# A mixture of experts whose tokens are gathered for two experts at a time, and an eighth weight buffer

## The chip, the cores and the metric

The kernel runs on one core of a Trainium2 chip. The metric is the device time of one execution in microseconds (us). The profile names the engines PE (TensorE, matmul; PEld are its weight loads, which overlap), DVE (VectorE), ACT (ScalarE), POOL (GpSimd) and SP (SyncE, which here only issues transfers).

## The reference

Three transformer blocks of width 1024 run one after another on one sequence of 256 tokens. Only the end of the third, a mixture of 32 experts of which each token uses four, bears on the change:

```python
def moe_ffn(h, router_w, router_b, w1, b1, w2, b2):
    logits = (h @ router_w + router_b).astype(jnp.float32)
    top_val, top_idx = lax.top_k(logits, TOP_K)      # 4 of 32
    gate = jax.nn.softmax(top_val, axis=-1)
    ...                                              # tokens are sorted by expert
    def block_ffn(args):
        xb, e = args
        act = clamped_swiglu(xb @ w1[e] + b1[e])     # 1024 -> 2 x 1024 -> 1024
        return act @ w2[e] + b2[e]                   # 1024 -> 1024
    ...
    contrib = gate_sorted[:, None].astype(h.dtype) * y_buf[dest]
    return jnp.zeros((T, D), h.dtype).at[sorted_tok].add(contrib)
```

All is float32. One expert's weights are 12 MB (8 for w1, 4 for w2), so all 32 are 384 MB that have to be read once.

## The kernel before

The blocks 1 and 2 and the mixer of block 3 take the first 1.7 ms and are not touched. `moe` then sorts the experts by how many tokens chose them. The first four in this order (`BIGS = 4`) are "large" and get up to 128 slots for tokens, the other 28 are "small" and get 64 (`SMALLS`). What doesn't fit is done by a fallback at the end, under a condition.

**Precision.** A float32 product is made of one-pass products of type `F32R`, on values split in a high and a low part. Weights: `split` (L507) copies a buffer of 1 MB ([128, 2048]) to `whi` on ScalarE (L509) and puts the difference into `wlo` on VectorE (L510). A large expert takes three products for each buffer (x high with w high, x high with w low, x low with w high); a small one puts the high and the low parts of its 64 tokens side by side in 128 columns and takes two. For a small expert one buffer in `up` and one in `down` (k == 1) is not split but multiplied as it is, as a plain float32 matmul.

**The loop.** Round r (0 to 31) runs `up(r)`, the first product of expert r (8 buffers, slots 0 to 7 of the round), and then `down` (4 buffers, slots 8 to 11) of the expert one (large) or two (small) earlier. The order on TensorE, ScalarE and VectorE is the order in which the program writes the instructions. All side work is put into slots: `at(r, slot, f)` says behind which buffer of which round `f` is written, and `pair_of(step, r, slot, behind)` writes a step's matmuls in a slot and its copy out of PSUM `behind` slots later. Such side work is the activation of the last pair of experts (`take`, `fold`, `activate`, `silu`, `gated`, `turn`), weighing the results by the gates (`weigh`), adding them to the tokens (`combine`), and the gather of the next experts' tokens.

**The gather.** `gather(r, n)` (L1753) makes the inputs of `n` experts from expert r on. `G` is a one-hot matrix (tokens by slots), built on VectorE. For each of 8 chunks of 128 features, `chunk(k)` multiplies the tokens (`hh` high, `hl` low, two halves of tokens each: four matmuls, each with weights of its own) by `G`, into one PSUM tile `gp` of the two `aux` banks, and ScalarE copies `gp` to `gx`. The matmuls' moving side is all `n` experts at once: 2 x 128 or 4 x 64, 256 columns. `scatter` transposes `G` of one expert for the way back and picks the gates. The calls: `gather(0, 2)` ahead of the loop (L1966), `gather(2, 2)` in one piece between `up(0)` and the bias products of round 0 (L2038 to L2040), `gather(4, 4)` in the slots of round 3, and from round 6 on `gather(r + 2, 4)` in every fourth round, slots 8 to 11 and then 0 to 7 of the next round.

**The weight buffers.** `raw` inside `moe` (L1794) issues each transfer of 1 MB on SyncE's queue, in order, into seven buffers in turn: five of tag `raw`, then `rawm`, then `rawx`. A transfer waits until the buffer's last readers are done. `gx` has three buffers of 8 KB per partition; the staging tile `braw` of the bias (L1969) uses one of them before its turn.

Of the kernel before, what the change touches and what calls it, by code (L numbers as in the profile page):

```python
# [12 lines left out]
F32 = mybir.dt.float32  # L13
F32R = mybir.dt.float32r
BF16 = mybir.dt.bfloat16
AF = mybir.ActivationFunctionType
# [10 lines left out]
UNIT = 1024  # L27
WAIT = 6
RAWS = 5
BIGS = 4  # L30
SMALLS = 64
# [294 lines left out]
class Norm:  # L326

    urgent = warm = False
    tag = "aux"
# [105 lines left out]
class Net:  # L435
# [1202 lines left out]
    def moe(s, x, nm, ctx):  # L1638


        nc, I = s.nc, s.I
        mm = nc.tensor.matmul
        mod = s.mods["wmod"]
        mp = ctx.enter_context(s.tc.tile_pool(name="mp", bufs=1))
# [64 lines left out]
        for t in range(2):  # L1709
            for i in range(2):  # L1710
                p = aux("htp", (128, 4, 128))
# [12 lines left out]
        p = aux("gatp", (128, 2, 128))  # L1724
# [4 lines left out]
        p = aux("gater", W)  # L1729
# [5 lines left out]
        X, GT, GS, Y, A = {}, {}, {}, {}, {}  # L1735
# [14 lines left out]
                nc.vector.tensor_reduce(GS[r], g, axis=AX.X, op=ALU.add)  # L1750
            return out

        def gather(r, n):  # L1753


            G = mp.tile([128, 2, n, 128], F32R, name="G", tag="G", bufs=1)
            slots, w = ("iota", 128) if n == 2 else ("twice", SMALLS)
            for t in range(2):
                for a in range(n):
                    nc.vector.tensor_scalar(G[:, t, a], k_(slots), pos[:, t, r + a:r + a + 1], None,  # L1760
                                            op0=ALU.is_equal)
            xg = [mp.tile([128, 8, 2, 128], F32R, name="gx", tag="gx", bufs=3) for _ in range(2)]
            for a in range(n):
                X[r + a] = (xg[a][:, :, 0], xg[a][:, :, 1]) if n == 2 else xg[a // 2][:, :, a % 2]

            def chunk(k):
                p = aux("gp", (128, n, 2, w))
                for i, src in enumerate((hh, hl)):
                    for t in range(2):
                        mm(p[:, :, i], src[:, t, k * 128:(k + 1) * 128], G[:, t, :, 0:w], start=t == 0,  # L1770
                           stop=t == 1)

                def out():
                    for a in range(2):
                        q = p[:, a] if n == 2 else p[:, 2 * a:2 * a + 2].rearrange("p a b c -> p a (b c)")
                        nc.scalar.activation(xg[a][:, k], q, AF.Copy)
                return out
            return [lambda k=k: chunk(k) for k in range(8)] + [lambda a=a: scatter(r + a, G[:, :, a])
                                                               for a in range(n)]

# [12 lines left out]

        def raw(ap):  # L1794

            s.turn = (s.turn + 1) % (RAWS + 2)
            if s.turn > 1:
                return s.raw(ap)
            if s.turn:
                w = s.xp.tile([128, 2 * UNIT], F32, name="rawx", tag="x", bufs=2)  # L1800
            else:
                w = mp.tile([128, 2 * UNIT], F32, name="rawm", tag="rawm", bufs=1)
            nc.sync.dma_start(w, ap)
            return w
        s.turn = 1

        def parts(what, r, k):

# [25 lines left out]
        def pair_of(step, r, slot, behind=2):  # L1834

            at(r, slot, lambda: at(r, slot + behind, step()))
# [126 lines left out]
            o = acc[:, 2 * c2:2 * c2 + 2]  # L1963
            return lambda: nc.vector.tensor_add(o, o, p)  # L1964

        for f in gather(0, 2):  # L1966
            f()()
        b1 = mp.tile([128, 1024], F32R, name="b1")
        b = mp.tile([128, 1024], F32, name="braw", tag="gx", bufs=3)  # L1969
        nc.scalar.dma_start(b, I["b1"])  # L1970
        b2 = s.xp.tile([32, 1024], F32, name="b2", tag="macc", bufs=1)
        nc.scalar.dma_start(b2, I["b2"])
# [22 lines left out]
        for r in range(32):  # L1995
            q = r - 1 if r < BIGS else r - 2

            d = {0: (), 1: (), BIGS: (BIGS - 2,), BIGS + 1: (), BIGS + 2: (BIGS - 1,)}.get(
                r, (r - 2,) if r < BIGS else (r - 3,))
            for z in d:  # L2000
                at(r, 1, lambda z=z: weigh(z, 0))
                at(r, 2, lambda z=z: weigh(z, 1))
                if z % 2:
                    for c2 in range(4):
                        pair_of(lambda z=z, c2=c2: combine(z - 1, c2), r, 4 + c2, 1)
            t = r - 1 if r <= BIGS else r - 2 if r % 2 == 0 else -1
            if t >= 0:
                at(r, 0, lambda t=t: activate(t))
                at(r, 1, lambda t=t: silu(t))
                at(r, 2, lambda t=t: gated(t))  # L2010

                def turned(t=t, r=r):
                    out = turn(t)
                    at(r, 6, lambda: out(0))
                    at(r, 7, lambda: out(1))
                at(r, 3, turned)
            if r != 0:
                at(r, 9 if r == BIGS else 10, lambda r=r: take(r))
                at(r, 9 if r == BIGS else 10, lambda r=r: fold(r, 0))
                at(r, 9 if r == BIGS else 11, lambda r=r: fold(r, 1))  # L2020
            if r == 3 or r % 4 == 2 and BIGS < r < 30:
                g = r + 1 if r == 3 else r + 2
                spots = [(3, k) for k in range(12)] if r == 3 else (
                    [(r, 8 + k) for k in range(4)] + [(r + 1, k) for k in range(8)])

                def begin(g=g, spots=spots):
                    for f, (rr, k) in zip(gather(g, 4), spots):
                        if (rr, k) == spots[0]:
                            at(rr, k + 2, f())
                        else:  # L2030
                            pair_of(f, rr, k)
                at(*spots[0], begin)
        order_ = s.tc.manual_schedule(engines={mybir.EngineType.PE, mybir.EngineType.Activation,
                                               mybir.EngineType.DVE})
        with order_:
            for r in range(32):
                up(r)
                if r == 0:  # L2038
                    for f in gather(2, 2):
                        f()()  # L2040
                    for c2 in range(4):
                        bias2(c2)
                    take(0)
                    for k in range(8, 12):
                        run(0, k)
                elif r < BIGS or r > BIGS + 1:
                    for _ in down(r - 1 if r < BIGS else r - 2, r):
                        pass
                elif r == BIGS:
                    half = down(BIGS - 1, r)  # L2050
                    next(half)
                    next(half)
                    run(r, 10)
                    run(r, 11)
                else:
                    run(r, 8)
                    run(r, 9)
                    for _ in half:
                        pass
                    run(r, 10)  # L2060
                    run(r, 11)
            activate(30)
            silu(30)
            weigh(29, 0)
            weigh(29, 1)
            gated(30)
            out = turn(30)
            for c2 in range(4):
                combine(28, c2)()
                if c2 % 2:  # L2070
                    out(c2 // 2)
            for _ in down(30, 32):
                pass
            xr = mp.tile([128, 8, T], F32, name="xr", tag="ml", bufs=1)
            nc.scalar.dma_start(xr, xd)
            d = down(31, 33, "up")
            next(d)
            weigh(30, 0)
            next(d)
            weigh(30, 1)  # L2080
            next(d)
            for c in range(8):
                nc.vector.scalar_tensor_tensor(acc[:, c], acc[:, c], g2(c), xr[:, c], op0=ALU.mult,
                                               op1=ALU.add)
            for _ in d:
                pass
            p = s.bank("cbl", (128, 4, 256), "p2", 1)
            ps = [p[:, 0:2], p[:, 2:4], aux("cbl", (128, 2, 256)), aux("cbl", (128, 2, 256))]
            for c in range(8):
                back(ps[c // 2][:, c % 2], c, (30,), c % 2 == 0, False)  # L2090
            weigh(31, 0)
            weigh(31, 1)
            for c in range(8):
                back(ps[c // 2][:, c % 2], c, (31,), False)
                nc.vector.scalar_tensor_tensor(acc[:, c], ps[c // 2][:, c % 2], g2(c), acc[:, c],
                                               op0=ALU.mult, op1=ALU.add)
                if c % 2:
                    nc.sync.dma_start(s.O["out"][:, c - 1:c + 1], acc[:, c - 1:c + 1])
# [49 lines left out]
    def past(s, mp, pgd, shift, acc, iota, hh, hl, g2):  # L2148
        nc, I = s.nc, s.I
# [3 lines left out]
        with s.tc.For_i(0, 32) as e:  # L2153
# [7 lines left out]
            q = aux("gto", (128, 2, 128))  # L2161
# [4 lines left out]
            q = aux("gso", (128, 1))  # L2166
            for t in range(2):
                mm(q, G[:, t], c4[:, 2 + t:3 + t], start=t == 0, stop=t == 1)
            nc.vector.tensor_copy(gs, q)
            xg = mp.tile([128, 8, 128], F32, name="xo", tag="gx", bufs=3)  # L2170
            for k in range(8):
                q = aux("xo", (128, 128))
                ks = slice(k * 128, k * 128 + 128)
# [34 lines left out]
            for k in range(8):  # L2208
                q = aux("bto", (128, 128))
# [61 lines left out]
```

## Time and profile before

| | us |
|---|---|
| median of 3 runs | 2808.79 |
| lowest and highest of them | 2794.71 and 2810.84 |
| the profiled execution, its own time | 2793.71 |
| its span in the trace | 2791.9 |

The profile is one execution. The page gives the busy time of each engine; the windows give it by stretch, with TensorE's granted clock (1.00 is full speed), the share of time that the transfers were busy, and their rate. The chain of work that ended last goes back from the last instruction: at each step to what released it, or to the instruction before it on its engine; "issue" in it is time in which the engine waited for nothing that the profile shows. Where two pieces of the chain follow each other without a gap on one engine, that engine set the pace there. The mixture of experts runs from some 1690 us to the end; the large experts up to about 1860 us.

### The profile page before, as it was taken

The page shows a single profiled execution, that of the slowest core. Times are in us where ns is not written, and L with a number is a line of the kernel's source. Part 1 is how long each engine was busy: PE and PEld are TensorE (multiplying, and loading weights), DVE is VectorE, ACT ScalarE, POOL GpSimd, SP SyncE. Part 2 cuts the span into 40 slices and gives each one's busy share as a digit, 9 for nine tenths or more (in the row PEclk, how much of TensorE's full clock was granted, in tenths as well). Part 3 has the DMA queues.
Part 4 walks back from the last instruction along what each step waited for, and adds up shares of the span by engine and source line. Part 5 has one row for each costly group of instructions (what it writes and reads, how often), then busy time and mean ns, then how long its engine had stood idle before and what let it go on. Part 6 is the DMA issues. An engine that isn't in the chain of part 4 may idle for free. (4 is left out here: it accounts for less than half of the span.)

```text
span 2791.9 us, 45884 instructions
## 1 busy us (share of the span) xinstructions
PE 2717.9 (97%) x17764; PEld 2364.8 (85%) x17764; DVE 2245.2 (80%) x3537; ACT 1683.1 (60%) x2658; POOL 3.3 (0%) x10
## 2 busy tenths in 40 slices
PE   9999999999999999999999998999999999999996
PEld 9999999999988999889999866877776767676764
DVE  7776777787776778888777754989999899999995
ACT  6554454464544545664467645777777777777773
POOL 0000000000000000000000000000000000000000
PEclk9999999999999999999999998999999999999998
DMA  7664466666653666437632333989999999999994
GB/s 290 229 227 166 173 221 240 244 224 242 227 182 122 236 243 225 150 139 256 234 142 96 111 118 120 359 306 384 395 405 395 398 402 389 405 387 400 388 413 161
DMA packets 102433, 728.97 MB, mean 261 GB/s; under 512 B 11384, under 2 KB 12920, under 8 KB 14528
## 3 DMA queue, kind: packets, MB, share of 16 engines
q1 hardware_dynamic: 99648, 719.64, 67.0%
q10 hardware_dynamic: 2560, 6.32, 0.7%
q8 instruction: 143, 2.34, 0.3%
q14 instruction: 82, 0.67, 0.1%
HBM read 723.80 MB, written 2.11 MB: 260 GB/s over the span
## 5 line engine op out<-in xcount | busy, mean ns | idle before, releaser
L510 DVE TENSOR_TENSOR wlo<-raw,whi 128x512 fp32r<-128x512 f32 (+1 forms) x1238 | 1178.7, 990 | 199.8 <-ACT whi L509 195.7
L509 ACT ACTIVATE whi<-raw 128x512 fp32r<-128x512 f32 (+1 forms) x1238 | 1006.6, 867 | 518.3 <-issue 283.1
L515 PE MATMUL gu<-xh,whi 128*128 128x256 f32 (+1 forms) x1760 | 499.7, 284 | 2.1 <-ACT whi L509 2.1
L517 PE MATMUL gu<-xh,wlo 128*128 128x256 f32 (+1 forms) x1760 | 497.6, 283 | 0.7 <-DVE wlo L510 0.7
L516 PE MATMUL gu<-xl,whi 128*128 128x256 f32 (+1 forms) x1760 | 498.1, 283 | 0.0
L515 PEld LDWEIGHTS gu<-xh,whi 128*128 128x128 f32 x1760 | 332.4, 189 | 2.9 <-ACT whi L509 2.5
L517 PEld LDWEIGHTS gu<-xh,wlo 128*128 128x128 f32 x1760 | 333.8, 190 | 1.1 <-DVE wlo L510 0.9
L516 PEld LDWEIGHTS gu<-xl,whi 128*128 128x128 f32 x1760 | 332.9, 189 | 0.3
L1848 PE MATMUL p<-whi,gx 128*128 128x512 f32 x1040 | 289.0, 404 | 2.5 <-ACT whi L509 2.5
L1848 PE MATMUL p<-wlo,gx 128*128 128x512 f32 x912 | 259.7, 407 | 23.6 <-DVE wlo L510 21.0
L517 PE MATMUL acc<-fh,wlo 128*128 128x256 f32 x880 | 245.5, 280 | 0.0
L516 PE MATMUL acc<-fl,whi 128*128 128x256 f32 x880 | 245.0, 280 | 0.1
L515 PE MATMUL acc<-fh,whi 128*128 128x256 f32 x880 | 242.4, 280 | 0.0
L1848 PEld LDWEIGHTS p<-whi,gx 128*128 128x128 f32 x1040 | 195.1, 189 | 54.5 <-issue 7.4
L1848 PEld LDWEIGHTS p<-wlo,gx 128*128 128x128 f32 x912 | 158.0, 189 | 78.7 <-DVE wlo L510 54.8
L516 PEld LDWEIGHTS acc<-fl,whi 128*128 128x128 f32 x880 | 165.8, 188 | 0.6 <-DVE fl L510 0.4
L517 PEld LDWEIGHTS acc<-fh,wlo 128*128 128x128 f32 x880 | 165.2, 188 | 0.0
L515 PEld LDWEIGHTS acc<-fh,whi 128*128 128x128 f32 x880 | 163.2, 187 | 1.2 <-ACT fh L509 0.8
L1870 PE MATMUL p<-whi,tp 128*128 128x512 f32 x464 | 154.0, 421 | 1.8 <-ACT whi L509 1.8
L1870 PE MATMUL p<-wlo,tp 128*128 128x512 f32 x400 | 128.8, 403 | 8.1 <-DVE wlo L510 8.1
L510 DVE TENSOR_TENSOR wlo<-rawm,whi 128x2048 fp32r<-128x2048 f32 x46 | 105.1, 2285 | 15.5 <-ACT whi L509 15.3
L1870 PEld LDWEIGHTS p<-whi,tp 128*128 128x128 f32 x464 | 87.1, 189 | 32.6 <-issue 11.5
(714 smaller groups left out, 5068.4 us busy)
## 6 DMA issues: line engine op xcount, KB each, us to landing
raw<-wmoe SPq DMA_DIRECT2D x276, 1024.0 KB, 7.9
raw<-wf SPq DMA_DIRECT2D x164, 1024.0 KB, 4.9
rawm<-wmoe SPq DMA_DIRECT2D x54, 1024.0 KB, 8.1
rawx<-wmoe SPq DMA_DIRECT2D x54, 1024.0 KB, 8.2
raw<-win SPq DMA_DIRECT2D x26, 1024.0 KB, 4.8
raw<-wada SPq DMA_DIRECT2D x24, 1024.0 KB, 4.8
raw<-wmod SPq DMA_DIRECT2D x24, 1024.0 KB, 5.1
raw<-wain SPq DMA_DIRECT2D x14, 1024.0 KB, 4.8
```

The costliest lines, as they stand in the source:

```text
L509: a = s.nc.scalar.activation(hi, x, AF.Copy)
L510: s.nc.vector.tensor_sub(lo, x, hi.bitcast(F32))
L515: mm(out, w[0], x[0], start=first, stop=False, skip_group_check=True)
L516: mm(out, w[0], x[1], start=False, stop=False, skip_group_check=True)
L517: mm(out, w[1], x[0], start=False, stop=last, skip_group_check=True)
L1848: mm(p[:, ns], xi, wi[:, ns], start=k == 0 and j == 0, stop=False, skip_group_check=True)
L1870: mm(p[:, n * 512:n * 512 + 512], xi, wi[:, c:c + 512], start=k == 0 and j == 0, stop=k == 7 and j == len(ts) - 1, skip_group_check=True)
```

## The change

The gather takes one expert at a time for the large ones and two for the small ones. `gx` has two buffers instead of three and one tile for each gather. The place of the third becomes an eighth weight buffer, `rawg`, the third in the turn after the five `raw`. Gathers now lie in round 0, 1, 2 and 3 (for the next expert, or for the first two small ones in round 3) and in every even round from 4 to 28; the piece between `up(0)` and the bias products is gone. `braw` lies in the tile of tag `ml`. In round 0 the copy out of PSUM follows one slot behind the matmuls, elsewhere two.

```diff
-        def gather(r, n):
+        def gather(r):
+            n = 1 if r < BIGS else 2
             G = mp.tile([128, 2, n, 128], F32R, name="G", tag="G", bufs=1)
-            slots, w = ("iota", 128) if n == 2 else ("twice", SMALLS)
+            slots, w = ("iota", 128) if n == 1 else ("twice", SMALLS)
...
-            xg = [mp.tile([128, 8, 2, 128], F32R, name="gx", tag="gx", bufs=3) for _ in range(2)]
+            xg = mp.tile([128, 8, 2, 128], F32R, name="gx", tag="gx", bufs=2)
             for a in range(n):
-                X[r + a] = (xg[a][:, :, 0], xg[a][:, :, 1]) if n == 2 else xg[a // 2][:, :, a % 2]
+                X[r + a] = (xg[:, :, 0], xg[:, :, 1]) if n == 1 else xg[:, :, a]
...
                         mm(p[:, :, i], src[:, t, k * 128:(k + 1) * 128], G[:, t, :, 0:w], start=t == 0,
                            stop=t == 1)
-                def out():
-                    for a in range(2):
-                        q = p[:, a] if n == 2 else p[:, 2 * a:2 * a + 2].rearrange("p a b c -> p a (b c)")
-                        nc.scalar.activation(xg[a][:, k], q, AF.Copy)
-                return out
+                return lambda: nc.scalar.activation(xg[:, k], p.rearrange("p a b c -> p (a b c)"), AF.Copy)
...
-            s.turn = (s.turn + 1) % (RAWS + 2)
-            if s.turn > 1:
+            s.turn = (s.turn + 1) % (RAWS + 3)
+            if s.turn > 2:
                 return s.raw(ap)
-            if s.turn:
+            if s.turn == 2:
+                w = mp.tile([128, 2 * UNIT], F32, name="rawg", tag="rawg", bufs=1)
+            elif s.turn:
...
-        s.turn = 1
+        s.turn = 2
...
-        for f in gather(0, 2):
+        for f in gather(0):
             f()()
-        b = mp.tile([128, 1024], F32, name="braw", tag="gx", bufs=3)
+        b = mp.tile([128, 1024], F32, name="braw", tag="ml", bufs=1)
...
-            if r == 3 or r % 4 == 2 and BIGS < r < 30:
-                g = r + 1 if r == 3 else r + 2
-                spots = [(3, k) for k in range(12)] if r == 3 else (
+            if r < BIGS or r % 2 == 0 and r < 30:
+                g = r + 1 if r < BIGS else r + 2
+                spots = [(r, k) for k in range(12)] if r < BIGS else (
                     [(r, 8 + k) for k in range(4)] + [(r + 1, k) for k in range(8)])
                 def begin(g=g, spots=spots):
-                    for f, (rr, k) in zip(gather(g, 4), spots):
+                    for f, (rr, k) in zip(gather(g), spots):
...
-                            pair_of(f, rr, k)
+                            pair_of(f, rr, k, 2 if rr else 1)
...
                 if r == 0:
-                    for f in gather(2, 2):
-                        f()()
```

## Rows read from the trace of the kernel before

**Rows 1.** The page: the span, and each engine's busy time with its share

```profile
span 2791.9 us, 45884 instructions
PE 2717.9 (97%) x17764; PEld 2364.8 (85%) x17764; DVE 2245.2 (80%) x3537; ACT 1683.1 (60%) x2658; POOL 3.3 (0%) x10
```

**Rows 2.** Windows: stretch, length, busy of each engine (instructions), PEclk, DMA share, GB/s

```profile
1760.00:1780.00 20.00, 20.00 (x88) 16.30 (x87) 18.87 (x12) 13.74 (x10) 0.00 (x0) 1.00 0.98 375
...
1970.56:2031.74 61.18, 59.25 (x241) 41.58 (x240) 57.85 (x38) 45.05 (x32) 0.00 (x0) 1.00 0.96 392
2031.74:2097.39 65.65, 64.22 (x290) 47.46 (x289) 60.10 (x50) 50.69 (x52) 0.00 (x0) 1.00 0.98 403
...
2650.00:2700.00 50.00, 48.25 (x205) 34.65 (x204) 47.87 (x32) 37.76 (x26) 0.00 (x0) 1.00 1.01 422
```

**Rows 3.** Waits, 1980 us to the end: engine, line, releaser: us, times, longest

```profile
ACT yh L1945 <- PE p L1870: 83.5, 25, 8.9
DVE wlo L510 <- ACT whi L509: 50.3, 50, 1.6
...
ACT whi L509 <- DMA raw<-wmoe: 12.2, 6, 3.1
...
ACT whi L509 <- DMA rawx<-wmoe: 3.0, 1, 3.0
...
ACT whi L509 <- DMA rawm<-wmoe: 2.8, 2, 2.3
```

**Rows 4.** Chain of work, 1700 us on: start, us, what; pair starts among them

```profile
1887.34 10.15 PE p L1848 x36
...
1903.96 1.95 issue
...
1970.56 2.26 issue
...
2667.47 2.26 issue
```

**Rows 5.** Chain, second half of a pair with a gather

```profile
2061.42 1.67 PE p L1870 x6
...
2073.56 4.35 PE p L1848 x12
...
2079.78 1.85 PE p L1848 x8
2081.63 0.47 PE gp L1770 x4
...
2083.95 0.22 PE gtp L1742 x2
2084.17 0.12 PE gtp L1744 x2
...
2091.20 0.02 issue
```

**Rows 6.** Chain, second half of a pair without a gather

```profile
2143.52 1.40 DVE wlo L510
...
2152.46 1.21 PE p L1848 x4
```

**Rows 7.** Timeline, weight loads: eight transposes (start, us, engine, line, operation, shape)

```profile
2110.86 0.97 PEld L1923 LDWEIGHTS atp<-const,ml 128*128 128x128 f32 x8
```

**Rows 8.** Timeline, TensorE between round 0 and round 1

```profile
1726.59 0.42 PEld L1770 LDWEIGHTS gp<-G,hh 128*128 128x128 f32 x2
...
1733.86 5.72 PE L1990 MATMUL b2p<-gT,b 32*128 32x256 f32 x16
...
1742.06 0.79 PE L1848 MATMUL p<-whi,gx 128*128 128x512 f32 x1 [2.48 <-ACT whi L509]
```

More of the change, by code (lines that the diff above doesn't have):

```diff
@@ L2169, in past @@
             nc.vector.tensor_copy(gs, q)
-            xg = mp.tile([128, 8, 128], F32, name="xo", tag="gx", bufs=3)
+            xg = mp.tile([128, 8, 128], F32, name="xo", tag="gx", bufs=2)
             for k in range(8):
```

## The prediction
> **What bounds the kernel now.** I read the busy times first, then one stretch at a time, then the waits, and last the chain of work. On the page TensorE shows 97% and VectorE 80% [rows 1], but those are averages over three blocks and a mixture of experts, and the change touches the last part alone. The stretches show what is special there: one round of two small experts moves 24 buffers of 1 MB (25.17 MB) and lasts 61.18 or 65.65 us, with the transfers busy 0.96 to 0.98 of the time [rows 2]. So three things could set the pace: transfers, VectorE (57.9 of 61.2 us) and TensorE.
>
> The waits sort them. From 1980 us on ScalarE, the first consumer of every weight buffer, waited for a transfer 9 times, 18.0 us in 812 us (12.2 + 3.0 + 2.8). VectorE waited for ScalarE 50 times, 50.3 us, and ScalarE waited 83.5 us for the end of a `down` product on TensorE [rows 3]. The weights are mostly there when they are wanted.
>
> The chain shows it by place. It is periodic: pairs of rounds without a gather take 61.18 us, pairs with one 65.65 us [rows 2]. Eleven pairs (8 to 29) lie between the starts 1970.56 and 2667.47, 696.9 us [rows 4]; five with a gather and six without would be 695.3. So at most 1.6 us of these eleven pairs is irregular, where late transfers would show. In a pair without a gather the second half of the chain goes along VectorE's splits (`wlo`) [rows 6]. In a pair with one, it is TensorE without a gap from 2061.42 to 2091.20: products, and between them eight times 0.47 us of gather (`gp`, four matmuls) and four times 0.22 + 0.12 us of scatter [rows 5]. That is 3.76 + 1.36 = 5.12 us of work, of which 65.65 - 61.18 = 4.47 us lengthens the pair and 0.65 us is hidden. **TensorE bounds exactly the stretch in which the gather lies.** That is what decides this change.
>
> **The change part by part.** *An eighth weight buffer.* `raw` issues each transfer once the buffer used eight units ago, not seven, is free. It can take away waits for transfers: at most the 1.6 us above and, for the pair that starts at 1903.96, 66.6 - 65.65 = 0.95 us. The sum takes this gain whole, since it counts no irregular time after the change.
>
> *Two experts instead of four.* ScalarE's copies stay eight of 256 columns per pair of small experts (before: sixteen per four), VectorE's `G` stays two per expert, the scatters one per expert. The matmuls do not stay. Before, a chunk had four matmuls of 256 columns for four experts; after, four matmuls of 128 columns for two. So the count per expert doubles: 32 per pair instead of 32 per four experts. Let c be the time of the four matmuls of a chunk. A pair with a gather of two then costs 8c + 2 x 0.34 - 0.65 = 8c + 0.03 us above 61.18, and every pair from 4 to 29 has one (13) where six pairs did.
>
> No row shows this matmul: a one-pass 4-byte product (`F32R`) of 128 columns. From below, each of the four loads its own weights, and eight 128-column transposes, which load as much, take 0.97 us, 0.12 each [rows 7]; the 256-column product takes 0.47/4 = 0.12. Halving columns cannot get much under that if the load sets it: c = 0.47. From above, the plain 4-byte product needs four passes: twelve instructions in 4.35 us, of which four one-pass ones take 1.85/2 = 0.93, leave 3.42 for eight, 0.428 each, and two of these make one product of 512 columns [rows 5]. For 128 columns that is 0.214, c = 0.856. Lower still, if nothing but columns counted, c = 0.235. I take c = 0.856: the one-pass pace is shown only for 256 columns and more, and the type is 4 bytes wide like the plain one. This choice is the weak point; all three values stay in the range or among the rivals.
>
> *Small experts.* The twelve pairs 6 to 29 took 2667.47 - 1903.96 = 763.5 us [rows 4]. After: 12 x (61.18 + 6.85 + 0.03) = 816.7, so +53.2. In pair 4 and 5 only some 10 us of chain are TensorE products [rows 4], so I charge half the gather, 3.4 (an estimate).
>
> *Large experts.* TensorE is busy all 20.0 of 20 us there [rows 2], so added matmuls add time. In round 0 the block of `gather(2, 2)` goes: from 1726.59 to 1733.86 it stood alone between `up(0)` and the bias products [rows 8], -7.27. Its end had also held back ScalarE's first split of round 1 (2.48 us of wait), which moves up with it. In exchange `gather(1)` runs within `up(0)`, +8c = 6.85; `gather(0)` keeps its 32 matmuls, now narrow, 8 x (0.856 - 0.47) = +3.1 (its ScalarE copies halve, hidden behind TensorE); rounds 1 and 2 get a gather each, 2 x (6.85 + 0.34) = +14.4; round 3 has two experts instead of four, 6.85 + 0.68 - 5.12 = +2.4. Together +19.5.
>
> `braw` in the place of `ml` costs nothing: its copy is in slot 3 of round 0, `take(0)` comes after `up(0)`, and up(0)'s products cover the time between; without this cover `take(0)` would wait for a copy of about a microsecond. No engine's queue gets a new wait but TensorE's: `gp` still waits for the copy two chunks back in the two `aux` banks, and the products of the next unit stand behind it.
>
> **Sum:** 53.2 + 3.4 + 19.5 = +76.1 on the profiled execution's 2793.7 us, 2870 us. That execution lies 15 us (0.5%) under the median of the three runs, beside the lowest of them; I let the upper end of the range take these 15 us in.
>
> **The rivals.** *B, the weight load sets the narrow matmul* (c = 0.47; for it: the transposes' 0.12; against it: nothing but that transposes multiply nothing). Pairs 64.97 us, 12 x 64.97 - 763.5 = +16.1; pair 4 and 5 +1.9; large experts 3.76 - 7.27 + 8.2 - 0.7 = +4.0. 2816 us, within 1%.
>
> *C, the matmul goes by its columns* (the other side: not slower; c = 0.235). It needs weight loads that get faster than any of [rows 5, 7] shows. Pairs 63.09 us, -6.4; +0.9; large experts -5.4: 2783 us. The break-even lies near c = 0.31: above that gathering in twos costs time. The Trainium skill's "TensorE: Matmul & The Clock Gate", section "Back-to-back issue gap", gives about 81 ns for each load and matmul of 128 columns in a stream. With that, c = 0.324 and the sum would be 2795 us, an estimate from that page; the 0.12 us of the transposes disagrees, and no row shows the thing itself.
>
> *D, buffers were the limit after all* (for it: the transfers' share of 0.96 to 0.98; against it: 18 us of waits, and a period that repeats). Were every pair paced by transfers at the 422 GB/s of the best stretch [rows 2], 25.17 MB would take 59.6 us, 12 pairs 47.8 us less: 2746 us. It decides only where TensorE's stretch is itself late for lack of weights, and [rows 5] shows it without a gap.
>
> **How the numbers follow.** My forecast (c near 0.86) 0.55, B 0.28, C with its 0.324 variant 0.10, D 0.05, something slower unforeseen 0.02. Within about 1% (28 us) a measurement of this kernel can't tell a change from none. Slower by more than 1%: 0.55, a fifth of B (if the shape of the pairs costs 7 us more than worked out) 0.05, and 0.02: 0.62. Within 1%: the rest of B and C, 0.32. Faster: D and a little of C, 0.06. The predicted time is the likeliest case's, 2870 us; its own range is 2850 to 2895. To hold 8 in 10 the range goes down over B: 2800 to 2895.
>
> **What would show each step.** The spacing of `gp` matmuls in the trace of after: 0.21 us each (forecast), 0.12 (B), 0.06 to 0.08 (C). The period of the pairs: all alike at 68, 65 or 63 us. ScalarE's waits for transfers should all but vanish, without the time following. Round 1's first product should start some 7 us sooner after the end of `up(0)`. The prediction is wrong if the narrow matmul costs no more than 0.12, or if pairs fall to 61 us or less: then the buffer was worth more than the chain shows.

## The result and the profile after

The changed kernel takes 2834.5 us (median of 7 runs, 2820.0 to 2836.3), the kernel before 2798.1 us (7 runs, the three of the table above among them): a ratio of 1.0113, 95% interval [1.0094, 1.0132]. Run again with other experiments it gave 1.0093 [1.0065, 1.0121]. It is about 1% slower. The forecast was 2870 us (+2.7%): the direction is right, the size is not.

The page of the changed kernel, span and busy times; [rows 1] answers to it:

```profile
span 2834.0 us, 46382 instructions
PE 2760.1 (97%) x18052; PEld 2411.4 (85%) x18052; DVE 2244.8 (79%) x3537; ACT 1684.4 (59%) x2658; POOL 3.3 (0%) x10
```

TensorE has 288 more instructions, VectorE and ScalarE as many as before. All pairs of small experts are now alike. Windows of the changed kernel, one pair of rounds with its gather (columns as in [rows 2], whose two pairs it answers to):

```profile
2004.75:2069.00 64.25, 62.83 (x282) 46.47 (x281) 58.85 (x44) 47.97 (x42) 0.00 (x0) 1.00 0.96 393
```

Chain of the changed kernel, second half of a pair; [rows 5] answers to it:

```profile
2162.94 1.65 PE p L1868 x6
2164.59 0.40 PE gp L1771 x4
...
2171.18 1.91 PE p L1868 x8
2173.09 0.40 PE gp L1771 x4
2173.48 0.98 PE p L1846 x4
...
2187.89 4.70 PE p L1846 x20
2192.59 0.93 PE p L1852 x4
2193.52 0.02 issue
```

TensorE still bounds this half without a gap, but a chunk of four narrow products takes 0.40 us, not 0.856. (One pair of the profile is an exception: its chain leaves TensorE at 2115.44 for a transfer of 9.45 us. The pair is no longer than the others.) The products around a chunk are a little slower than beside a wide one: eight take 1.91 us where [rows 5] has 1.85.

One thing is not of the change. The first gather product starts at 1709.8 us in this profile and at 1696.6 us before, because TensorE's granted clock was 0.70 on average from 1620 to 1660 us, in code that both kernels share (1.00 before; in the repeat of the changed kernel, e1_again, 1.00, and its first product at 1701.3). So the stages are counted from there. A stretch runs from the start of one expert's bias products (`p<-b,er`, the end of its `up`) to that of another; the kernels beyond the first two are told below.

| us, stretch | before | after | e4_bank | e7_wide0 | e9_round3 |
|---|---|---|---|---|---|
| first gather product to bias of 0 | 29.3 | 37.0 | 37.0 | 32.7 | 32.7 |
| bias 0 to 1 | 41.1 | 44.4 | 38.4 | 39.0 | 38.8 |
| 1 to 2 | 35.0 | 39.2 | 39.2 | 39.2 | 39.2 |
| 2 to 4 | 76.9 | 76.4 | 76.4 | 76.4 | 77.7 |
| 4 to 6 | 53.9 | 61.7 | 60.3 | 61.7 | 53.5 |
| 6 to 30 (12 pairs) | 762.5 | 770.9 | 771.0 | 770.9 | 770.9 |
| 30 to the end | 96.5 | 94.6 | 95.2 | 94.5 | 94.9 |
| all | 1095.3 | 1124.2 | 1117.5 | 1114.3 | 1107.6 |

The repeat gives 1124.4, so this count repeats much better than whole times do. The change costs 28.9 us, 1.0%, and the twelve pairs, for which I had forecast 53, have 8.4 of it. Most, 22.4 us, is lost ahead of round 6, around the large experts and in rounds 4 and 5, in stretches that I had priced by the same wrong c or not seen at all.

### The profile page after: what moved, and what is told of

Its sections match the earlier page's. It is cut to its first block, busy times and chain, and to the rows that moved or that the text cites. A ratio compares the mean times of both kernels' runs of the same rounds, so it can differ in the third digit from the quotient of the medians.

```text
span 2834.0 us, 46382 instructions
## 1 busy us (share of the span) xinstructions
PE 2760.1 (97%) x18052; PEld 2411.4 (85%) x18052; DVE 2244.8 (79%) x3537; ACT 1684.4 (59%) x2658; POOL 3.3 (0%) x10
## 4 chain that ended last, share of the span: by engine, by line
PE 77%; DVE 11%; issue 7%; ACT 4%; DMA 1%; ACTq 0%; DVEq 0%
PE p L1846 11%; PE gu L515 7%; PE gu L517 7%; PE gu L516 7%; DVE wlo L510 6%; PE p L1868 6%; PE acc L515 5%; PE acc L517 5%; PE acc L516 5%; ACT whi L509 3%; PE gp L1771 2%; DVE acc L1962 1%; DVE tp L1933 1%; DVE ml L1909 1%; DVE ml L1884 1%
## 5 line engine op out<-in xcount | busy, mean ns | idle before, releaser
L510 DVE TENSOR_TENSOR wlo<-raw,whi 128x512 fp32r<-128x512 f32 (+1 forms) x1216 | 1128.6, 966 | 196.2 <-ACT whi L509 192.6
L509 ACT ACTIVATE whi<-raw 128x512 fp32r<-128x512 f32 (+1 forms) x1216 | 966.7, 848 | 502.9 <-issue 286.3
L510 DVE TENSOR_TENSOR wlo<-rawg,whi 128x2048 fp32r<-128x2048 f32 x47 | 107.5, 2287 | 29.1 <-ACT whi L509 29.1
```

Of the source, the lines that this page charges most:

```text
L509: a = s.nc.scalar.activation(hi, x, AF.Copy)
L510: s.nc.vector.tensor_sub(lo, x, hi.bitcast(F32))
```

## The experiments

**e1_again**: the changed kernel itself, unchanged.

> The changed kernel once more, for a second profile. In the first one its logits (lt, L1635) come at 1690.3 us against 1676.8 before, 13.5 us late ahead of any changed line, with TensorE's granted clock at 0.63 and 0.77 from 1620 to 1660. Theory A (this lag belongs to one execution and not to the change): the second profile has lt within 3 us of 1677 or at another place, and its time is lower by as much, 2818 to 2826 us, while the rest of the delays (round 0 +8, rounds 4 and 5 +7, pairs +7.5) stay. Theory B (the change moves it, for instance by addresses): lt again at 1690, the time again 2835.

Measured: 2825.9 us, ratio 1.0093; pairs 64.25 us; 1124.4 us from the first gather product to the end. It separates what repeats (every stage of the table within 1.6 us, but for the last, 97.1 us against 94.6) from the lag ahead of the change, which does not: theory A.

**e2_seven**: the changed kernel with seven weight buffers.

```
-            s.turn = (s.turn + 1) % (RAWS + 3)
-            if s.turn > 2:
+            s.turn = (s.turn + 1) % (RAWS + 2)
+            if s.turn > 1:
...
-        s.turn = 2
+        s.turn = 1
```

> The gather as changed, but seven weight buffers as before; the eighth's place is empty. Theory A (TensorE paces every pair now, the buffer is worth nothing): the pairs stay at 64.25 us, the total within 4 us of the changed kernel. Theory B (the buffer works and hides part of what the gather costs): pairs of 65 us and more with ScalarE waiting for transfers, the total 10 to 25 us longer. Theory C (the eighth buffer itself disturbs): some us shorter.

Measured: 2826.7 us, ratio 1.0091 [1.0060, 1.0121]; pairs 64.25 us. All waits of ScalarE's splits for transfers from 1980 us on, the changed kernel's and then this one's; [rows 3] answers to both:

```profile
ACT whi L509 <- DMA raw<-wmoe: 0.5, 1, 0.5
```

```profile
ACT whi L509 <- DMA raw<-wmoe: 3.5, 4, 2.7
```

The buffer takes away 3 us of waiting that nobody waited for: in the changed kernel its gain is nothing. Rival D falls, and with it the 1.6 and 0.95 us that I had let the sum take. That these waits would all but vanish came true, 18.0 us before and 0.5 after, but most of it isn't the buffer's, since seven have only 3.5. What an eighth would do beside the old gather no run shows.

**e3_wide**: the small experts' chunks widened to 256 columns again, half of them thrown away.

```
+                c = 128 if n == 2 else w
-                p = aux("gp", (128, n, 2, w))
+                p = aux("gp", (128, n, 2, c))
-                        mm(... G[:, t, :, 0:w] ...)
+                        mm(... G[:, t, :, 0:c] ...)
...
```

> The changed kernel, but the matmuls of the small experts' gathers stream 256 columns again (each expert's 64 twice, the second half not copied out); their number stays that of the change. Theory A (a gather matmul costs mostly by being one, 0.10 us at 128 columns against 0.12 at 256): a chunk goes from 0.40 to 0.47 us, pairs from 64.25 to 64.8, the total +6 to +8 us. Theory B (columns decide): a chunk doubles, pairs at 67.5, the total +40.

Measured: pairs 64.41 us, ratio 1.0104 [1.0057, 1.0150]. Chain of this kernel, second half of a pair:

```profile
2160.48 0.47 PE gp L1772 x4
2160.95 1.86 PE p L1872 x8
```

A chunk costs 0.07 us more, as in theory A, but the products behind it 0.05 us less, which theory A had not seen (64.8 expected). Halving the columns saved 0.16 us a pair.

**e10_twice, e11_split, e12_less**: the slope of the sum, from the changed kernel: each small product issued twice; each split into two of 64 columns; half of them left out, so that half of the tokens are not gathered.

```
-                    for t in range(2):
+                    for t in range(2) if n == 1 else (0, 1, 0, 1):     (e10)
+                    for t in range(2 if n == 1 else 1):                (e12)
-                        mm(p[:, :, i], ..., G[:, t, :, 0:w], ...)
+                        mm(p[:, a, i], ..., G[:, t, a, 0:w], ...)      (e11, for a in range(n))
...
```

> The changed kernel with each of the four products of a small expert pair's chunk issued twice (the second time over the first, same result): 8 products of 128 columns for 4, everything else the same. It measures the slope of the prediction's sum, in which a pair takes 61.2 us and eight chunks of c each. Theory (TensorE bounds the half of the pair in which the chunks lie): pairs go from 64.25 to 67.3 to 67.6 us (8 x 0.40 more), the 12 pairs 38 us longer. Rival (the half is bound by ScalarE or VectorE once the gather is in it, and the products have slack): pairs stay below 65.5.

> The changed kernel with each product of a small expert pair's chunk split into two of 64 columns, one for each expert: 8 products for 4, the same columns in all. Theory (a narrow product is priced by the product, its weight load and its start, no longer by its columns): it costs what e10_twice costs, a chunk about 0.8 us, pairs 67 us or more. Rival (priced by columns, 0.10 us for 128): a chunk stays near 0.40 us and pairs within 0.5 us of 64.25.

> The changed kernel with half of the gather's products of the small experts left out (the second half of the tokens is not gathered): 2 products for 4 in each chunk, the copies and everything else as they are. Theory (slope one also downwards): pairs take 62.5 to 62.8 us, 64.25 less 8 x 0.20, the 12 pairs 18 to 20 us shorter, and the whole then comes to within 0.4 per cent of the kernel before. Rival (the copies ahead of the splits, not the products, make the 3 us by which a pair with a gather is longer): pairs stay above 63.7.

Chains, second half of a pair, of e10_twice, e11_split and e12_less:

```profile
2176.60 0.84 PE gp L1771 x8
2177.44 1.91 PE p L1868 x8
```

```profile
2173.23 0.81 PE gp L1772 x8
2174.04 1.94 PE p L1869 x8
```

```profile
2167.07 0.17 PE gp L1771 x2
2167.24 1.91 PE p L1868 x8
```

Pairs take 67.77 us with eight products of 128 columns in a chunk, 67.80 with eight of 64, 64.25 with four, 62.50 with two (means of twelve). Up and down the slope is the same: 3.52/32 and 1.75/16, 0.11 us for each product, with 64 columns as with 128. **A narrow product is priced by the piece, not by the column**, and TensorE does bound that half, since every product added or left out moves the pair. e12_less as a whole stands at 1.0015 [0.9993, 1.0038]: without half of the small gather's products the loss is within what can be measured.

What sets the price is seen in the weight loads. Timeline of e11_split, weight loads of one chunk, then the first one behind it:

```profile
2173.07 0.41 PEld L1772 LDWEIGHTS gp<-G,hh 128*128 128x128 f32 x3
2173.40 0.53 PEld L1772 LDWEIGHTS gp<-G,hl 128*128 128x128 f32 x4
2173.85 0.19 PEld L1869 LDWEIGHTS p<-whi,tp 128*128 128x128 f32 x1
```

Seven loads from 2173.07 to 2173.85 are 0.11 us each, and the products of 64 columns start as far apart. In the changed kernel the loads of `gp` are 0.11 us apart too (median), and so are those of the scatter's products with 2 columns. All of these load 128 columns. Elsewhere in the profile of the changed kernel, at a granted clock of 1.00, a load goes by its columns: the next one follows a load of 64 columns after 0.055 us (`pv<-pT,vb`, at 1622.52) and one of 32 after 0.028 (`lgt<-h,rw`, at 1677.94). So the 0.11 us is the load of 128 columns, and these products go at its pace.

**e4_bank**: the two steps that hold the end of expert 1's gather run ahead of the products that start the accumulator (`bias2`, in the trace `b2p`).

```
                 if r == 0:
+                    run(0, 8)
+                    run(0, 9)
                     for c2 in range(4):
                         bias2(c2)
```

> The changed kernel, but slots 8 and 9 of round 0 (the copies that free the two aux banks of the gather) are written ahead of the bias products b2p, not behind them. Theory A (one of two banks is held through b2p, so TensorE waits 0.69 us for ScalarE four times): b2p goes back to some 5.7 us without these waits, round 1 starts 2 to 4 us sooner, the total 2 to 5 us lower. Theory B (the 12.2 us between up(0) and up(1) come from the lower granted clock there, 0.79): no change beyond 1 us.

Measured: 2822.5 us, ratio 1.0075 [1.0047, 1.0103]; from bias 0 to 1 38.4 us instead of 44.4 (42.8 in the repeat). Timeline of TensorE behind `up(0)`, first the changed kernel, then e4_bank; [rows 8] answers to both:

```profile
1746.80 1.09 PE L1852 MATMUL p<-b,er 128*128 128x512 f32 x4
1747.82 1.13 PE L1988 MATMUL b2p<-gT,b 32*128 32x256 f32 x4
1749.63 1.12 PE L1988 MATMUL b2p<-gT,b 32*128 32x256 f32 x4 [0.69 <-ACT acc L1989]
1751.44 1.88 PE L1988 MATMUL b2p<-gT,b 32*128 32x256 f32 x4 [0.69 <-ACT acc L1989]
1754.01 2.07 PE L1988 MATMUL b2p<-gT,b 32*128 32x256 f32 x4 [0.69 <-ACT acc L1989]
1756.76 0.69 PE L1742 MATMUL gtp<-const,G 128*128 128x128 f32 x2 [0.69 <-ACT acc L1989]
...
1759.94 2.07 PE L1846 MATMUL p<-whi,gx 128*128 128x512 f32 x4 [2.27 <-ACT whi L509]
```

```profile
1734.77 1.08 PE L1852 MATMUL p<-b,er 128*128 128x512 f32 x4
...
1736.12 3.80 PE L1988 MATMUL b2p<-gT,b 32*128 32x256 f32 x16
1742.40 2.08 PE L1846 MATMUL p<-whi,gx 128*128 128x512 f32 x4 [2.48 <-ACT whi L509]
```

Since the copy of `gather(1)`'s last chunk, and its scatter, were left until after the `b2p` products, those had one `aux` bank for their four turns instead of two, and TensorE waited 0.69 us for ScalarE before each of three turns and again before the scatter. With the steps moved the sixteen run in one piece. The four waits are 2.8 us of the gain. The rest goes with the clock, so theory B had a part in it: behind `up(0)` the granted clock stood at 0.50 for 17.1 us in the changed kernel (13.7 in the repeat) and for 10.2 in e4_bank, as in the kernel before. Half of the difference, 3.4 us (1.8 in the repeat, an estimate), is about what the waits leave of 6.0 (4.4).

**e7_wide0**: e4_bank with expert 0's gather alone widened to 256 columns.

```
+            m = 2 if r == 0 else n
-            G = mp.tile([128, 2, n, 128], ...)
+            G = mp.tile([128, 2, m, 128], ...)
...
```

> The kernel of e4_bank with expert 0's gather alone widened to 256 columns again (its one-hot columns are written twice side by side, ScalarE copies the first half of the result only): the kernel before gathers two experts of 128 columns there. In e4_bank from the first gp product to the bias products of up(0) pass 36.99 us, with TensorE's granted clock at 0.50 for some 12 to 14 us; the kernel before needs 29.3 us and shows 0.50 for about 3 us only. Theory (the clock stays at half because TensorE starts the stage on narrow products): with the wide ones the clock is back at 1.00 within 5 us, as before, and the stretch takes 30 to 32 us (0.56 us more for eight chunks of 0.47, and gather(1)'s chunks in up(0) stay), the whole 5 to 6 us faster than e4_bank. Rival (the clock falls there whatever the width, and what brings it back before is that products of 512 columns are mixed in from the third chunk on): the stretch stays at 36 to 38 us and the whole within 1 us of e4_bank.

Measured: 2816.5 us, ratio 1.0066 [1.0043, 1.0090]; first gather product to bias 0 32.65 us, not 36.99 (30 to 32 expected). Windows of the first products of round 0 (behind the five engines stands the granted clock), of the kernel before, the changed one and e7_wide0:

```profile
1699.00:1702.00 3.00, 3.00 (x12) 2.48 (x11) 0.00 (x0) 0.66 (x2) 0.00 (x0) 0.62 0.28 105
1702.00:1705.00 3.00, 3.00 (x22) 2.57 (x22) 0.00 (x0) 2.24 (x8) 0.00 (x0) 1.00 0.00 0
```

```profile
1712.00:1715.00 3.00, 3.00 (x16) 3.00 (x15) 0.00 (x0) 1.21 (x4) 0.00 (x0) 0.50 0.00 0
1715.00:1718.00 3.00, 3.00 (x16) 2.90 (x15) 0.57 (x3) 1.48 (x4) 0.00 (x0) 0.50 0.00 0
1718.00:1721.00 3.00, 3.00 (x11) 2.71 (x12) 0.53 (x3) 0.17 (x1) 0.00 (x0) 0.50 0.03 5
1721.00:1724.00 3.00, 3.00 (x8) 2.32 (x8) 0.00 (x0) 0.21 (x1) 0.00 (x0) 0.50 0.01 3
```

```profile
1699.00:1702.00 3.00, 3.00 (x17) 3.00 (x16) 0.00 (x0) 1.39 (x4) 0.00 (x0) 0.54 0.00 0
1702.00:1705.00 3.00, 3.00 (x23) 2.64 (x22) 1.11 (x6) 1.27 (x4) 0.00 (x0) 1.00 0.02 5
```

In all three the clock falls to its lower level (0.50, 1.2 GHz) shortly after the gather begins, behind a stage of small products with gaps (in each of the three TensorE idles 0.97, then 0.81, then 0.52 us just ahead of it). With wide products it is back in 3 to 4 us (6.8 in e8_before_early, where the fall came ahead of the first one), with narrow ones it stays at 0.50 for 13.7, in every run that has them, and the products of `up(0)` behind them run at half speed too. The change put narrow products in a place where the clock was about to fall.

**e5_late**: e4_bank with the gather that is begun in round 4 moved whole into round 5.

```
+                if r == BIGS:
+                    spots = [(r + 1, k) for k in range(10)]
```

> The kernel of e4_bank (the changed kernel with steps (0,8) and (0,9) run ahead of the bias products), and the gather that is begun in round 4, the first of two small experts, is put whole into round 5, steps 0 to 9, so that in ScalarE's order its copies no longer stand ahead of the weight splits that round 5's first products wait for. In the changed kernel's trace two of those copies wait 1.74 and 2.86 us for TensorE, VectorE then waits 3.29 us for ScalarE's rounding, TensorE 1.13 us for VectorE, and from the bias products of round 4 to those of round 5 pass 31.0 to 31.8 us where the kernel before has 23.9. Theory (the place of the copies in ScalarE's queue costs round 5 its time): that stretch falls by 4 to 6 us, the idle time of VectorE before the splits there goes, and the whole gets about 5 us faster than e4_bank (some 2817 us, ratio about 1.006). Rival (the stretch is longer because TensorE has half a gather more in it, and the stall is only the sign of it): the gather's four moved chunks add 4 x 0.40 us to round 5, the stretch stays at 31 us or grows to 32.5, and the whole is 0 to 2 us slower than e4_bank.

Measured: ratio 1.0098 [1.0063, 1.0132]. From bias 4 to 5 28.3 us instead of 30.4, from 5 to 6 33.2 instead of 29.9: 1.2 us worse in all. Of the rival's numbers the whole came out, but not the stretch (31 us or more expected), and its reason wasn't settled: in round 5 too ScalarE's copies stand ahead of the splits, with waits for TensorE of 3.1 and 2.6 us. The next one tries another place.

**e9_round3**: e7_wide0 with that gather moved the other way, to right behind the one of round 3.

```
+                if r == BIGS:
+                    spots = [(r - 1, 10), (r - 1, 11)] + [(r, k) for k in range(8)]
```

> e7_wide0 with the gather that is begun in round 4 (experts 6 and 7) moved two steps after the other one of round 3: steps (3,10), (3,11) and (4,0) to (4,7), so that rounds 5 and 6 have none in front of their splits. Theory (in e5_late the same copies only moved in front of other splits of round 5, and what costs there is the place ahead of a split, not the 3.2 us of products): from the bias products of round 3 to those of round 6 pass 95.1 us in e7_wide0 (33.4, 31.8, 29.9) and 88.0 in the kernel before; here they take 90 to 92, and the whole is 3 to 5 us faster than e7_wide0, ratio about 1.005. Rival (any place costs the same, since the stretch is full): 95 us again, the whole within 1 us of e7_wide0.

Measured: from bias 3 to 6 88.2 us instead of 95.1, 0.2 more than the kernel before has. The ratio, 1.0063 [1.0042, 1.0084], can't tell it from e7_wide0; counted from the first gather product it is 6.7 us shorter. Timeline behind round 4, ScalarE with VectorE and TensorE in the repeat of the changed kernel, and then ScalarE in e9_round3:

```profile
1901.52 0.38 ACT L1773 ACTIVATE gx<-gp 128x256 fp32r<-128x256 f32 x1 [1.74 <-PE gp L1771]
1904.76 0.39 ACT L1773 ACTIVATE gx<-gp 128x256 fp32r<-128x256 f32 x1 [2.86 <-PE gp L1771]
1905.04 1.90 ACT L509 ACTIVATE whi<-raw 128x2048 fp32r<-128x2048 f32 x1
...
1906.98 2.29 DVE L510 TENSOR_TENSOR wlo<-raw,whi 128x2048 fp32r<-128x2048 f32 x1 [3.29 <-ACT whi L509]
1907.00 1.85 PE L1846 MATMUL p<-whi,gx 128*128 128x512 f32 x4 [1.13 <-ACT whi L509]
```

```profile
1889.64 1.91 ACT L509 ACTIVATE whi<-raw 128x2048 fp32r<-128x2048 f32 x1
1891.44 1.90 ACT L509 ACTIVATE whi<-rawm 128x2048 fp32r<-128x2048 f32 x1
1893.25 1.90 ACT L509 ACTIVATE whi<-rawx 128x2048 fp32r<-128x2048 f32 x1
```

A copy that waits for TensorE holds back the rounding of weights that lie ready, and both VectorE's split (3.29 us) and TensorE's products (1.13 us) wait for that rounding. Without the copies there the roundings follow one another. The Trainium skill says of ScalarE's and VectorE's queues, in "PSUM — Partial Sum Buffer", section "Engine vs sequencer instructions", that they are strictly first in, first out; the rows agree.

e9_round3 moves the gather's products and its copies together, so it shows the place and doesn't part the two. In rounds 3 and 4, too, the copies stand ahead of splits, but there the eight wait 1.6 us for TensorE in all, against 7.6 in e4_bank and 9.0 in the changed kernel. So it is the wait of the copy that goes with the loss, not its place alone. The products have some part: issued twice (e10_twice) they lengthen the stretch from bias 4 to 5 from 30.4 us in e4_bank to 32.6 (the granted clock is 1.00 throughout in both), less than the 3.5 us that 32 of them cost in a pair. So has the clock: in the changed kernel it stood at 0.50 for 3.4 us in that stretch, in e4_bank not, which is 1.4 us shorter there (0.6 shorter than the repeat).

**e6_early**: e4_bank with e5_late's edit, and half of every later gather moved into the first half of the pair, where TensorE has idle time. **e8_before_early**: the same on the kernel before, with its gathers of four.

```
-                    [(r, 8 + k) for k in range(4)] + [(r + 1, k) for k in range(8)])
+                    [(r, k) for k in range(4)] + [(r, 8 + k) for k in range(4)] + [(r + 1, k) for k in range(4)])
...
```

> The kernel of e4_bank with e5_late's place for the first small gather, and every later gather of two begun earlier: its chunks 0 to 3 in steps (r,0) to (r,3) of the even round with their copies one step behind, chunks 4 to 7 in steps (r,8) to (r,11), the scatters in (r+1,0) and (r+1,1). Nothing else changes, the work on each engine is the same. Theory (TensorE sets the time only from the middle of a pair, where it is full and the gather's eight chunks lie, and VectorE sets it in the first half, where TensorE has idle time): four chunks of 0.40 us go where they cost nothing, a pair falls from 64.25 us to 62.4 to 62.8 (the pairs without a gather of the kernel before have 61.18), and 12 pairs are 17 to 22 us faster, the whole some 2798 us with e5_late's part, ratio about 0.999. Rival (in the first half the order of ScalarE and VectorE is as tight: the copies of 0.38 us each delay the splits there as much as the products are relieved): pairs stay within 0.4 us of 64.25, the whole within 5 us of e5_late. A third way (transfers: a pair moves 25.2 MB, and at the 417 GB/s of a full stretch that is 60.4 us) could stop the gain only near 60.5 us.

> The kernel BEFORE, gathers of four as they were, with the small gathers begun earlier as in e6_early: chunks 0 to 3 in steps (r,0) to (r,3) with the copies one step behind, 4 to 7 in (r,8) to (r,11), the four scatters in (r+1,0) to (r+1,3). It asks whether what e6_early gains belongs to the change or is to be had without it. Theory of e6_early: the six pairs with a gather fall from 65.65 us to about 63.5, the six without stay at 61.18, 12 to 14 us less, the whole some 2786 us, ratio about 0.995, and so faster than both kernels. Rival: pairs unchanged, ratio 0.999 to 1.001; or the copies (two of a chunk here) late and the pairs longer.

Both got slower: 1.0234 [1.0195, 1.0273] and 1.0082 [1.0057, 1.0108]. In e6_early the first half of most pairs grew from 33.0 to 36.8 us and the second shrank only from 31.2 to 31.0. ScalarE, then VectorE in that first half of e6_early:

```profile
2290.24 0.38 ACT L1773 ACTIVATE gx<-gp 128x256 fp32r<-128x256 f32 x1 [3.72 <-PE gp L1771]
2290.52 1.91 ACT L509 ACTIVATE whi<-raw 128x2048 fp32r<-128x2048 f32 x1
```

```profile
2285.98 2.29 DVE L510 TENSOR_TENSOR wlo<-rawg,whi 128x2048 fp32r<-128x2048 f32 x1 [2.08 <-ACT whi L509]
2292.46 2.29 DVE L510 TENSOR_TENSOR wlo<-raw,whi 128x2048 fp32r<-128x2048 f32 x1 [2.40 <-ACT whi L509]
```

Idle time of TensorE was there, but the copy that goes with each chunk isn't free in a half that VectorE and ScalarE set. The theory fell. In e8_before_early the half with the moved chunks grew too, from 33.0 to 33.8 us to 36.4 to 39.1. Not all of it is the copies: in both kernels TensorE's granted clock fell to 0.50 for 3.4 us in most of these halves. The three of e6_early without such a fall take 35.2 us, those with one 36.8 to 37.0; of the five of e8_before_early above, two without take 36.4 and 36.9, three with one 37.7, 38.3 and 39.1. No version that was run beats the kernel before.

## Why the prediction was right or wrong

*What bounds the stretch: right.* TensorE sets the half in which the gather lies, with a slope of one (e10_twice, e12_less). The eighth buffer is worth nothing in the changed kernel (e2_seven), which fits the 1.6 us that the irregular time had left it at most.

*The price of the narrow product: wrong, and this is the step that failed.* I took c = 0.856, from the pace of the plain 4-byte product, where the bounds were 0.235, 0.47 and 0.856. A chunk takes 0.40 us on the chain and 0.44 with the products behind it: rival B, whose row was the nearest, the eight transposes with their 0.97 us [rows 7]. They too load 128 columns of weights for 128 columns to multiply, while the plain product takes 0.856 us for 512 columns where a one-pass one takes 0.23. The width of the type was the weaker likeness. The sign I had named was plain: `gp` products start 0.11 us apart (0.11 is the median; behind the first of a chunk, whose weights were loaded ahead, it can be 0.06), against 0.12 for B and 0.21 for mine. Even B's 0.12 was a reading too high: the 0.97 us of [rows 7] is a merged line with a short gap in it and the whole of the last load, and its loads too stand 0.11 us apart.

The Trainium skill's "TensorE: Matmul & The Clock Gate" has two sections on this. "Back-to-back issue gap" (81 ns), which I cited, is below the 0.11 us measured. "LDWEIGHTS (loading the stationary operand)" gives P/1.2 ns for a load of P columns, 107 ns for 128 by an estimate from it: the trace agrees with that one, and with its shorter loads too.

*The pairs.* Their formula with c = 0.44 gives 61.18 + 3.52 + 0.03 = 64.73, measured 64.25: what is hidden of a gather was 1.1 us, not 0.65. Twelve pairs: +53.2 forecast. Measured by the chain, eleven pairs from 2004.75 to 2711.47 take 64.25 us each, twelve 771.0, against 763.5 of [rows 4]: +7.5 (+8.4 between the bias products of the table).

*The large experts.* With c = 0.44 the terms come to +3.3 for round 0 (3.52 for `gather(1)`, and 8 x (0.44 - 0.47) for the narrow `gather(0)`), to -7.27 + 3.5 = -3.8 from bias 0 to 1, and to +3.9 from 1 to 2. Measured: +7.7, +3.3 and +4.2. The last is right. In the first a step was missing, the clock: 4.3 us of it go with e7_wide0. In the second, too: the -7.27 counted the block's own time and not that its end had freed both `aux` banks for the `b2p` products. I had written that no queue but TensorE's gets a new wait; this was such a wait, in TensorE's queue, but not where I looked for it. With the lower clock behind it, it cost 4.4 to 6.0 us (e4_bank). Round 1's first product, announced 7 us sooner after `up(0)`, came 13.1 us after the start of `up(0)`'s bias products instead of 16.2, and 7.6 us after it in e4_bank.

*Rounds 4 and 5.* Charged with half a gather, 3.4 us; +7.7 measured, and e9_round3 takes all of it away, by another place for products and copies together. Most of it goes with ScalarE's copies that wait ahead of the splits, some with the clock; how much is each one's no run parts. I had counted the copies (as many as before) and not asked what stands behind each in the queue: that no queue but TensorE's gets a new wait was wrong of ScalarE's.

*So the size fell between the forecast and B by two errors of opposite sign.* The sum has 140 c in it (96 in the pairs, 4 in rounds 4 and 5, 40 around the large experts) and 43.8 us to be taken off: +17.8 with c = 0.44. The pairs hid 5.8 us more than that, which leaves +12.0. Three losses that I had not priced, 4.3 us of clock ahead of `up(0)`'s end, 6.0 of the held bank and 5.9 of the place of the gather in rounds 4 and 5 (the last two with some lower clock in them), bring it to 28.2; the count from the first gather product says 28.9. So close a sum is in part chance: the end behind round 30, 1.9 us shorter, stands in none of its terms. The direction rested on the right mechanism, but without these three the narrow products alone would have made less than the 1% that can be measured. That it came out clear of the noise was luck.

## What to carry to other kernels

Here splitting a batched matmul into narrower ones saved nothing below the price of its weight load, 0.11 us: count products, not columns, and take the price from the row that loads as many weights, not from the one with the same type. When work moves from a block of its own into a stream, ask for each of its copies what is queued behind it on its engine, and which bank it holds when the next user comes. And idle time of one engine is not free room for work that also needs another engine's queue: twice here it made the kernel slower.

## What was unexpected of the hardware

The product of 128 rows by 64 columns takes as long as that by 128: eight in 0.81 and 0.84 us. TensorE's granted clock stayed at 0.50 for 13.7 us while the engine was busy without a gap on narrow products and then on the first wide ones; widening the products to 256 columns brought it back in 3 to 4 us, although they do no more useful work.
